# A hybrid DeepNorm layer: TensorE's order of the hyena stage emitted by a count of work instead of by the scheduler

## Chip, cores, metric

One core of a Trainium2 chip runs the whole program. The metric is the device time of one execution, in microseconds, shown as the median of several runs. TensorE (PE) does the matrix products, VectorE (DVE) and ScalarE (ACT) the elementwise work, GpSimd (POOL) the subtractions that split weights, and SyncE (SP) issues nearly all loads and stores.

## What is computed

One encoder layer (sequence 1024, model width 1024, all float32). Two token mixers read one combined projection of the normalised input; the part that the change touches is the second, the hyena branch. Cut to that, the reference reads:

```python
h = _layer_norm(x) * (1.0 + scale) + shift
p = h @ w_in + b_in                      # q, k, v | gate | hyena | gate | merge gates
u = centred_conv3(p_hy, conv_w, conv_b)
v, x1, x2 = jnp.split(u, 3, axis=-1)
filters = implicit_filters(S, ...)       # 3 sine layers of width 64, a product with w4, a decay
z = v
for o, gate_o in enumerate((x1, x2)):
    z = gate_o * (bidirectional_long_conv(z, filters[:, o, 0], filters[:, o, 1]) + filt_bias[o] * z)
y_hy = z * jax.nn.silu(g_hy)
```

The long convolution is a circular one of size 2048 by Fourier transforms. Behind the branches come two projections, sigmoid merge gates from the same `p`, an output projection, and a second normalisation.

## The kernel before

Precision: every projection splits both factors into a high and a low part and makes three products, wh·hTh, wh·hTl and wl·hTh. One projection tile (128 output columns for all 1024 positions) is two halves of 8 k-tiles by three products, that is 48 matmuls of 128x512 (`proj`, matmul on L242). Its weights come by one 512 KB load on SP (`load_w`, L229), are rounded by ScalarE (L222) and subtracted by GpSimd (`split_w`, L223). Names in the rows: `pj` is the PSUM tile of a projection, `hTh`/`hTl` the split input, `wh`/`wl` the split weights.

Stages: normalisation and adaLN up to about 61 us of the span; the hyena stage, to about 657 us, where attention's first score product (L859, tile `ss`) is issued; attention; the output stage from about 1240 us.

The hyena stage holds, beside 28 projection tiles of its own (12 for the inputs x, 12 early merge gates, 4 output gates) and the first tiles of attention:

- `hidden`: the sine layers of the filters, for two halves of two directions. A product on TensorE (L357, L359), then a range reduction on VectorE and a sine on ScalarE (L362 to L368), three times; the last result is split into `hid` (L374, L375).
- `gen_filter`, four times, for channel half hc and order o: eight pairs of products `px` = hid·w4 (L560, L561), each multiplied on VectorE by a decay table `dk` (L563) that SP loads into one of two buffers (L556); then butterflies (L447, L459) and a forward transform in eight frequency groups, j = -1 to 6 (`split_product`: `z` on L509 for j = -1, on L521 else), whose results `hs` are stored.
- `conv_order`/`long_conv`, four times in a row, each fed by the one before: for each frequency group a forward product `z` (L531 in plain float32 for j = -1, else L521), a product with the filter's spectrum on VectorE (L625, L627, then L447), a split into `yh`, `yl` (L499 on ScalarE, L500 on VectorE, signs on L511 and L512), an inverse product (L521), and butterflies into the result, which multiplies x (L693).
- `conv_to_rows`: one x tile is projected, copied (L591, L596), filtered by eight shifted multiply-adds on VectorE (`y`, L608), and transposed on TensorE (L612) into `xx` (L613). `gate_r` projects an early merge gate, `silu_tile`/`out_gate` an output gate.

Order: the tile scheduler orders all engines. It takes the emission order below as priorities; `conv_order` stands in `tc.high_priority(offset=HIGH)`, so that the convolutions' instructions go first and projections fill between them. The fills are placed by the driving calls at L719 to L749 with FILLS = (3, 1, 4, 4) and GATES = (0, 3, 2), the numbers of early gates emitted at each place. The products' tables `tcon0` and `tcon` are loaded at L730 to L733, into memory that the filters' pools free.

## Time and profile before

| | us |
|---|---|
| median of 3 runs (lowest, highest) | 1461.28 (1456.95, 1463.21) |
| the profiled execution | 1466.4 |
| its span | 1464.6 |
| PE busy | 1351.3 (92%) |
| DVE busy | 957.6 (65%) |
| ACT busy | 624.4 (43%) |
| POOL busy | 282.2 (19%) |

The span is the time between the first and the last recorded instruction of the profiled execution; its own time is 1.8 us longer. Times in rows count from the span's start. Busy shares of TensorE are those of pipelined matmuls, so a matmul's own duration is longer than the distance between two of them.

### The profile page before, as it was taken

How to read it: one execution, taken by the hardware profiler on the slowest of the kernel's cores; microseconds unless marked ns; L12 is line 12 of the kernel's file. 1: busy time of each engine (PE TensorE's matmuls, PEld its weight loads, DVE VectorE, ACT ScalarE, POOL GpSimd, SP SyncE). 2: the span in 40 equal slices, each digit the busy share in tenths (PEclk: the TensorE clock that was granted, in tenths of full speed). 3: DMA queues.
4: the chain of work that ended last, by engine and by line, in shares of the span. 5: the costliest groups of instructions: out<-in, count | busy, mean ns of one | idle time of the engine just before them, and what ended most of it. 6: DMA issues, size and time to landing. Idle time of an engine off the chain costs nothing.

```text
span 1464.6 us, 18389 instructions
## 1 busy us (share of the span) xinstructions
PE 1351.3 (92%) x6707; PEld 1098.4 (75%) x6707; DVE 957.6 (65%) x1709; ACT 624.4 (43%) x1220; POOL 282.2 (19%) x160
## 2 busy tenths in 40 slices
PE   4788979889899999999999999999999999689997
PEld 1467767767777777788988788878887888567886
DVE  4798768767999898745156714761466144288866
ACT  1544444534244443446355534663466343242110
POOL 1221121210113122141121112111211111231220
PEclk9799999999999999999999999999999999899999
DMA  9633544332112222121113421311131114588523
GB/s 255 182 97 105 175 133 149 110 130 79 54 58 69 87 65 79 58 84 30 44 59 116 103 61 58 92 30 43 59 91 31 44 58 123 184 249 220 158 88 72
DMA packets 157024, 145.86 MB, mean 100 GB/s; under 512 B 16611, under 2 KB 126591, under 8 KB 156678
## 3 DMA queue, kind: packets, MB, share of 16 engines
q1 hardware_dynamic: 156486, 140.44, 32.7%
q0 software_dynamic: 288, 4.19, 0.8%
q8 instruction: 53, 0.87, 0.3%
q14 instruction: 37, 0.30, 0.1%
q10 hardware_dynamic: 160, 0.06, 0.0%
HBM read 116.73 MB, written 27.92 MB: 99 GB/s over the span
## 4 chain that ended last, share of the span: by engine, by line
PE 64%; DVE 11%; DMA 5%; ACT 3%; issue 2%; POOL 1%; SPq 0%; DVEq 0%; ACTq 0%; POOLq 0%
PE pj L242 33%; PE pj L888 6%; PE z L521 6%; PE po L1138 6%; PE pj L1103 4%; PE po L929 2%; PE pp L922 2%; DVE iv L447 2%; DVE f L447 1%; DMA dk<-in_t_dec 1%; DMA wor<-in_w_out 1%; PE z L531 1%; PE ss L859 1%; DVE f L459 1%; DVE q L447 1%
## 5 line engine op out<-in xcount | busy, mean ns | idle before, releaser
L223 POOL TENSOR_TENSOR wl<-wr,wh 128x1024 fp32r<-128x1024 f32 x88 | 234.8, 2668 | 966.9 <-ACT wh L222 895.7
L242 PE MATMUL pj<-hTh,wh 128*128 128x512 f32 x1024 | 407.5, 398 | 4.0 <-ACT hTh L433 4.0
L242 PE MATMUL pj<-hTl,wh 128*128 128x512 f32 x1024 | 407.1, 398 | 1.5 <-POOL hTl L435 0.8
L242 PE MATMUL pj<-hTh,wl 128*128 128x512 f32 x1024 | 408.1, 399 | 0.0
L242 PEld LDWEIGHTS pj<-hTl,wh 128*128 128x128 f32 x1024 | 194.3, 190 | 40.5 <-DVE hTl L435 2.2
L242 PEld LDWEIGHTS pj<-hTh,wh 128*128 128x128 f32 x1024 | 194.4, 190 | 39.9 <-ACT hTh L433 4.1
L242 PEld LDWEIGHTS pj<-hTh,wl 128*128 128x128 f32 x1024 | 194.4, 190 | 37.3 <-issue 1.0
L222 ACT CAST wh<-wr 128x1024 fp32r<-128x1024 f32 x88 | 92.4, 1050 | 239.5 <-PE pj L242 82.3
L499 ACT CAST yh<-f 128x512 fp32r<-128x512 f32 x88 | 54.1, 615 | 105.2 <-DVE f L447 93.9
L899 DVE TENSOR_TENSOR tmp<-pj,bv 128x512 f32<-128x512 f32 x16 | 11.1, 692 | 115.0 <-PE pj L888 115.0
L500 DVE TENSOR_TENSOR yl<-f,yh 128x512 fp32r<-128x512 f32 x88 | 65.6, 756 | 22.2 <-ACT yh L499 19.9
L521 PE MATMUL z<-yh,tcon 128*128 128x512 f32 x224 | 65.7, 411 | 8.6 <-ACT yh L499 8.6
L918 ACT ACTIVATE sx<-sx,stat 128x256 f32<-128x256 f32 (+1 forms) x128 | 71.6, 563 | 3.1 <-DVE stat L916 3.0
L916 DVE CUSTOM_DVE_ANT_0 sx<-ss,tab 128x384 f32<-128x384 f32 (+1 forms) x112 | 53.7, 492 | 29.2 <-PE ss L844 18.0
L888 PE MATMUL pj<-wh,hTh 128*128 128x256 f32 x256 | 72.7, 284 | 0.0
L888 PE MATMUL pj<-wl,hTh 128*128 128x256 f32 x256 | 72.6, 284 | 0.0
L888 PE MATMUL pj<-wh,hTl 128*128 128x256 f32 x256 | 72.6, 284 | 0.0
L925 DVE TENSOR_TENSOR pt<-pp,pt 128x256 fp32r<-128x256 f32 (+1 forms) x128 | 61.8, 486 | 14.9 <-ACT pt L924 13.6
L1103 PE MATMUL pj<-yh,wl 128*128 128x512 f32 x128 | 52.0, 406 | 17.8 <-ACT yh L1084 11.3
L924 ACT CAST pt<-pp 128x256 fp32r<-128x256 f32 (+1 forms) x128 | 52.2, 425 | 33.4 <-PE po L929 28.9
L922 PE MATMUL pp<-ident,sx 128*128 128x128 f32 x320 | 58.3, 280 | 4.2 <-DVE pt L925 2.7
L521 PEld LDWEIGHTS z<-yh,tcon 128*128 128x128 f32 x224 | 40.6, 191 | 22.3 <-ACT yh L499 15.0
(236 smaller groups left out, 2546.2 us busy)
## 6 DMA issues: line engine op xcount, KB each, us to landing
wr<-in_w_in SPq DMA_DIRECT2D x64, 512.0 KB
xt<-in_x SPq DMA_DIRECT2D x32, 256.0 KB
wa<-in_w_ada SPq DMA_DIRECT2D x16, 512.0 KB
dk<-in_t_dec SPq DMA_DIRECT2D x32, 256.0 KB
r_d<-thr SPq DMA_DIRECT2D x32, 256.0 KB
h_dram<-hs SPq DMA_DIRECT2D x32, 256.0 KB
ht<-h_dram SPq DMA_DIRECT2D x32, 256.0 KB
thr<-r_d SPq DMA_DIRECT2D x32, 256.0 KB
```

What stands on the lines that cost most here:

```text
L222: ACT.copy(wh[:, :k, :], src)
L223: PO.tensor_tensor(wl[:, :k, :], src, wh[:, :k, :].bitcast(F32), ALU.subtract)
L242: PE.matmul(ps, w[:, kt, :], h[:, kt, sl], start=i == 0, stop=i == len(ops) - 1)
L447: V.tensor_tensor(o, a, b, op)
L500: V.tensor_tensor(yl[:, c, :], y, yh[:, c, :].bitcast(F32), ALU.subtract)
L521: PE.matmul(z, m, v, start=k == 0, stop=k == 5)
L888: PE.matmul(ps[:, t % 2], h[:, 4 * q + k, P * t : P * t + P], w[:, 2 * k : 2 * k + 2, :], start=first and t % 2 == 0 and i == 0, stop=last ...
L918: ACT.activation(sx[:, : n * P], sx[:, : n * P], AF.Exp, bias=stat[:, t, e, 0:1], scale=-1.0, accum_out=stat[:, t, e, 1:2])
L922: PE.transpose(pp[:, a * P : (a + 1) * P], sx[:, a * P : (a + 1) * P], ident)
L925: V.tensor_tensor(pt[:, :n, 1, :], blk(pp), pt[:, :n, 0, :].bitcast(F32), ALU.subtract)
L1103: PE.matmul(ps, w[:, 4 * b + kt, :], y[:, kt, :], start=i == 0, stop=i == len(ops) - 1)
L1138: PE.matmul(po, m[:, P * q : P * q + P], w[:, kt, ds_], start=n == 0, stop=n == 23)
```

## The change

Around the hyena stage, TensorE's instructions are put under `tc.manual_schedule`: TensorE then issues them exactly in the order in which the program emits them, while the other engines are still ordered by the scheduler. The emission keeps two counts, `clk["pe"]` and `clk["dve"]`, of the work emitted so far for TensorE and for VectorE. Before each transform product and each filter product it calls `pace()`, which pulls projection work from a queue, three matmuls at a time, until TensorE's count reaches 1.1 times VectorE's plus 1 us. The queue is filled by `push_x`, `push_gates` and `push_out`; transposes of an x tile are put off to the next tile's middle. In `long_conv` the inverse product of group j - 1 and the butterflies of j - 2 are emitted behind the forward product of group j. `high_priority` and FILLS are gone, GATES holds six numbers. `split_w` takes an engine as an argument, and no call gives one, so the weight splits stay on GpSimd. The work itself is the same: the same products, loads and elementwise operations.

```diff
-FILLS = (3, 1, 4, 4)
-GATES = (0, 3, 2)
+
+GATES = (0, 4, 2, 2, 0, 4)
+RATIO = 1.1
+LAG = 1.0
...
+    def split_w(src, eng=None):
 
         k = src.shape[1]
+        eng = eng or PO
...
+    clk = {"pe": 0.0, "dve": 0.0}
+
+    def cols_of(ap):
+        n = 1
+        for k in ap.shape[1:]:
+            n *= k
+        return n
+
+    def dve(ap):
+        clk["dve"] += 0.14 + 0.001065 * cols_of(ap)
+
+    def pe(n, passes=1):
+        clk["pe"] += 0.0133 + passes * n / 2400
...
+    def prefetch(n0):
+        if n0 not in ready:
+            w = load_w(w_in[:, n0 : n0 + P])
+            ready[n0] = split_w(w)
+
+    def pull():
+
+        while now or queue:
+            if not now:
+                now.append(queue.pop(0)[1]())
+            if next(now[0], None):
+                return True
+            now.clear()
+        while deferred:
+            for _ in deferred.pop(0)():
+                pass
+        return False
+
+    def pace(lag=LAG):
+        while clk["pe"] < RATIO * clk["dve"] + lag and pull():
+            pass
+
+    def proj_steps(n0, evac):
+
+        prefetch(n0)
+        wh, wl = ready.pop(n0)
+        for half in range(2):
+            ps = ps_w.tile([P, 512], F32, name="pj", tag="mm")
+            sl = slice(512 * half, 512 * half + 512)
+            ops = [(w, h, kt) for kt in range(KT) for w, h in ((wh, hTh), (wh, hTl), (wl, hTh))]
+            for i, (w, h, kt) in enumerate(ops):
+                PE.matmul(ps, w[:, kt, :], h[:, kt, sl], start=i == 0, stop=i == len(ops) - 1)
+                pe(512)
+                if i % 3 == 2:
+                    yield True
+            if half == 0:
+                if queue:
+                    prefetch(queue[0][0])
+                while deferred:
+                    yield from deferred.pop(0)()
+            evac(half, ps, cols[:, BIN + n0 // P : BIN + n0 // P + 1])
...
-        def split_product(j, y, tab, inverse, pool):
-
-
-            z = ps_z.tile([P, 2, W], F32, name="z", tag="z")
+        def split_y(j, y, inverse, pool):
+
             yh, yl = [pool.tile([P, 3, W], F32R, name="y" + q, tag="y" + q, bufs=2) for q in "hl"]
             at = int(inverse)
             c, n = slice(at, at + 2), 2 - 2 * at
             ACT.copy(yh[:, c, :], y)
             V.tensor_tensor(yl[:, c, :], y, yh[:, c, :].bitcast(F32), ALU.subtract)
+            dve(y)
+            if j >= 0:
+                ACT.mul(yh[:, n, :], y[:, at, :], -1.0)
+                ACT.mul(yl[:, n, :], yl[:, 2 * at, :].bitcast(F32), -1.0)
+            return yh, yl
+
+        def split_product(j, parts, tab, inverse):
+
+
+            pace()
+            z = ps_z.tile([P, 2, W], F32, name="z", tag="z")
+            yh, yl = parts
...
+                    pace()
                     for m in range(2):
                         hs = hid[e][:, a // 2, P * m : P * m + P]
                         PE.matmul(px[:, m, :], hs, wh, start=True, stop=False)
                         PE.matmul(px[:, m, :], hs, wl, start=False, stop=True)
+                        pe(2 * W)
                     b = a + 8 * e
                     V.tensor_tensor(g[:, b : b + 2], px, dk, ALU.mult)
+                    dve(dk)
...
+            def turn():
+                if "x" not in x:
+                    x["x"] = pool.tile([P, 8, W], F32, name="xx", tag=tag, bufs=bufs)
+                for q in range(2):
+                    px = ps_x.tile([P, 512], F32, name="px", tag="px")
+                    for a in range(4):
+                        PE.transpose(px[:, a * P : (a + 1) * P], y[:, (4 * q + a) * P : (4 * q + a + 1) * P], ident)
+                        pe(P, 2)
+                    ACT.copy(x["x"][:, 4 * q : 4 * q + 4, P * c : P * c + P], px.rearrange("p (a c) -> p a c", a=4))
+                    yield True
+                x["left"] -= 1
+
+            deferred.append(turn)
...
-                v = conv_product(j, p1, True)
+                return p1
+
+            def inverse(j, p):
+                v = conv_product(j, conv_split(j, p, True), True)
...
+            r, p = {}, None
+            for j, y in stage1(x[:, 0:4], x[:, 4:8], x, quad("s"), quad("d"), quad("q")):
+                z = conv_product(j, conv_split(j, y, False), False)
+                if j >= 0:
+                    inverse(j - 1, p)
+                if j > 0:
+                    butterflies(j - 2)
+                p = spectrum(j, z)
+            inverse(6, p)
+            butterflies(5)
+            butterflies(6)
...
         def conv_order(x, z, hc, o):
 
-            with tc.high_priority(offset=HIGH):
-                for a, y in long_conv(z, hc, o):
-                    V.tensor_tensor(x[:, a], y, x[:, a], ALU.mult)
-            return x
-
-        def out_gate(z, hc):
-            for c in range(2):
+            for a, y in long_conv(z, hc, o):
+                xt = need(x)
+                V.tensor_tensor(xt[:, a], y, xt[:, a], ALU.mult)
+                dve(y)
+            return need(x)
...
-        x0 = conv_x(0, 0)
-        gen_filter(0, 0)
-        x1 = conv_x(0, 1)
-        gen_filter(0, 1)
-        fill(GATES[0])
-        gen_filter(1, 0)
-        fill(GATES[1])
-        gen_filter(1, 1)
-        fill(GATES[2])
...
-        z = conv_order(x1, x0, 0, 0)
-        x2 = conv_x(0, 2, "xx2")
-        fill(FILLS[0])
-        z = conv_order(x2, z, 0, 1)
-        x0 = conv_x(1, 0)
-        x1 = conv_x(1, 1)
...
+        with tc.manual_schedule(engines={PE.engine}):
+            clk.update(pe=0.0, dve=0.0)
+            x0 = push_x(0, 0)
+            push_gates(GATES[0])
+            x1 = push_x(0, 1)
+            push_gates(GATES[1])
+            for hc, o in ((0, 0), (0, 1), (1, 0), (1, 1)):
+                gen_filter(hc, o)
+                note(("filter", hc, o))
+            need(x1)
+            fpool.close()
+            hy = st.enter_context(tc.tile_pool(name="hy", bufs=1, reuse_waits="tile", side="right"))
+            tcon0 = hy.tile([P, 8, P], F32, name="tcon0")
+            SY.dma_start(tcon0, A["t_con0"])
+            tcon = hy.tile([P, 28, P], F32R, name="tcon")
+            PO.dma_start(tcon, A["t_con"])
+            hy2 = st.enter_context(tc.tile_pool(name="hy2", bufs=2, reuse_waits="tile", side="right"))
+            x2 = push_x(0, 2, "xx2")
+            push_gates(GATES[2])
+            z = conv_order(x1, need(x0), 0, 0)
+            note("conv 0 0")
+            x0 = push_x(1, 0)
+            push_gates(GATES[3])
+            z = conv_order(x2, z, 0, 1)
+            note("conv 0 1")
+            x1 = push_x(1, 1)
+            need(x0)
+            og = push_out(z, 0)
+            push_gates(GATES[4])
+            x2 = push_x(1, 2, "xx2")
+            z = conv_order(x1, need(x0), 1, 0)
+            note("conv 1 0")
+            need(og)
+            push_gates(GATES[5])
+            z = conv_order(x2, z, 1, 1)
+            note("conv 1 1")
+            push_out(z, 1)
+            push_gates(N_EARLY)
+            while pull():
+                pass
```

Three places on TensorE, as the order of instructions shows them. In these rows a line number, the operation, what it writes and reads, and the tile's size stand; "x4" is four alike in a row.

The sine layers, before: TensorE around the third pair of products (L359), with projection matmuls (`pj`) of the first x tiles and early gates and the transposes of the first x tile (L612) between them.

```order
L242 MATMUL pj<-hTh,wl 128x512
L242 MATMUL pj<-hTh,wh 128x512
L359 MATMUL px<-f,w_124 128x512
L242 MATMUL pj<-hTl,wh 128x512
L242 MATMUL pj<-hTh,wl 128x512
L242 MATMUL pj<-hTh,wh 128x512
L242 MATMUL pj<-hTl,wh 128x512
L359 MATMUL px<-f,w_124 128x512
L612 MATMUL px<-ident,y 128x128 x4
L242 MATMUL pj<-hTh,wl 128x512
```

The same place with the change: the last matmuls of the first projection, all six sine-layer products (L407, L409), and the first filter products.

```order
L288 MATMUL pj<-hTl,wh 128x512
L288 MATMUL pj<-hTh,wl 128x512
L407 MATMUL px<-feat,w_125 128x512 x2
L409 MATMUL px<-f,w_124 128x512 x4
L630 MATMUL px<-w4h,hid 128x256
L631 MATMUL px<-w4l,hid 128x256
L630 MATMUL px<-w4h,hid 128x256
L631 MATMUL px<-w4l,hid 128x256
L288 MATMUL pj<-hTh,wh 128x512
```

Ahead of the first filter product (`px<-w4h,hid`) TensorE had 153 projection matmuls and 16 transposes; now it has 9 projection matmuls and none of the transposes.

The products of the first filter, before: a stretch of the eight pairs, with fills of projection matmuls.

```order
L560 MATMUL px<-w4h,hid 128x256
L561 MATMUL px<-w4l,hid 128x256
L242 MATMUL pj<-hTh,wh 128x512
L242 MATMUL pj<-hTl,wh 128x512
L242 MATMUL pj<-hTh,wl 128x512
L242 MATMUL pj<-hTh,wh 128x512
L242 MATMUL pj<-hTl,wh 128x512
L242 MATMUL pj<-hTh,wl 128x512
L242 MATMUL pj<-hTh,wh 128x512
L242 MATMUL pj<-hTl,wh 128x512
L242 MATMUL pj<-hTh,wl 128x512
L242 MATMUL pj<-hTh,wh 128x512
```

With the change, in the same eight pairs:

```order
L630 MATMUL px<-w4h,hid 128x256
L631 MATMUL px<-w4l,hid 128x256
L288 MATMUL pj<-hTh,wh 128x512
L288 MATMUL pj<-hTl,wh 128x512
L288 MATMUL pj<-hTh,wl 128x512
L630 MATMUL px<-w4h,hid 128x256
L631 MATMUL px<-w4l,hid 128x256
L630 MATMUL px<-w4h,hid 128x256
L631 MATMUL px<-w4l,hid 128x256
```

The eight pairs now hold three fills of 3 projection matmuls in this filter, and two of 3 in each of the other three, where fills of 1 to 12 stood.

The end of the second convolution, before: TensorE at a forward product (six matmuls, four with `yh` and two with `yl`), an inverse product behind it, the fill, and the next pair.

```order
L242 MATMUL pj<-hTl,wh 128x512
L242 MATMUL pj<-hTh,wl 128x512
L242 MATMUL pj<-hTh,wh 128x512
L521 MATMUL z<-yh,tcon 128x512 x4
L521 MATMUL z<-yl,tcon 128x512
L242 MATMUL pj<-hTl,wh 128x512
L242 MATMUL pj<-hTh,wl 128x512
L242 MATMUL pj<-hTh,wh 128x512
L521 MATMUL z<-yl,tcon 128x512
L242 MATMUL pj<-hTl,wh 128x512
L242 MATMUL pj<-hTh,wl 128x512
L242 MATMUL pj<-hTh,wh 128x512
```

The end of the same convolution with the change: forward 5, inverse 4, forward 6, inverse 5 and inverse 6.

```order
L583 MATMUL z<-yh,tcon 128x512 x4
L583 MATMUL z<-yl,tcon 128x512 x2
L583 MATMUL z<-yh,tcon 128x512 x4
L583 MATMUL z<-yl,tcon 128x512 x2
L583 MATMUL z<-yh,tcon 128x512 x4
L583 MATMUL z<-yl,tcon 128x512 x2
L583 MATMUL z<-yh,tcon 128x512 x4
L583 MATMUL z<-yl,tcon 128x512 x2
L583 MATMUL z<-yh,tcon 128x512 x4
L583 MATMUL z<-yl,tcon 128x512 x2
L288 MATMUL pj<-hTh,wh 128x512
```

The last five products follow each other with no projection between them, since the queue was empty there; the 72 projection matmuls come behind them.

## Rows read from the trace of the kernel before

**Rows 1.** Windows view, the filter part of the stage: busy, clock, DMA share, GB/s.

```profile
115.90:302.30 186.40, 163.02 (x748) 131.04 (x747) 143.14 (x210) 83.89 (x161) 35.41 (x21) 0.94 0.46 147
```

**Rows 2.** Timeline, the bounds of the three parts: start us, us, engine, line.

```profile
61.43 0.79 PE L242 MATMUL pj<-hTh,wh 128*128 128x512 f32 x1 [4.01 <-ACT hTh L433]
...
115.91 0.41 PE L560 MATMUL px<-w4h,hid 128*128 128x256 f32 x1
...
302.31 3.75 PE L531 MATMUL z<-f,tcon 128*128 128x256 f32 x8 [5.06 <-DMA tcon<-in_t_con]
...
657.07 0.28 PE L859 MATMUL ss<-ks,qs 128*128 128x256 f32 x1
```

**Rows 3.** Timeline of TensorE, fill behind a forward product and the next product.

```profile
485.48 0.39 PE L242 MATMUL pj<-hTh,wl 128*128 128x512 f32 x1
...
489.12 0.39 PE L521 MATMUL z<-yh,tcon 128*128 128x512 f32 x1
```

**Rows 4.** Timeline of TensorE, eight transposes of an x tile.

```profile
113.62 1.07 PE L612 MATMUL px<-ident,y 128*128 128x128 f32 x8 [2.63 <-DVE y L608]
```

**Rows 5.** Windows view of VectorE in the sine chain.

```profile
79.60:110.20 30.60, 30.43 (x56) 1.00 0.37 116
```

**Rows 6.** Groups by line of VectorE, 79 to 110 us: busy, mean ns.

```profile
L608 DVE SCALAR_TENSOR_TENSOR y<-u,cols,y 128x192 f32<-128x192 f32 (+3 forms) x13 | 8.1, 641 | 0.0
```

**Rows 7.** Timeline of VectorE behind the sine chain.

```profile
108.78 1.39 DVE L375 TENSOR_TENSOR hid<-f,hid 64x512 fp32r<-64x512 f32 x2
...
117.01 0.69 DVE L563 TENSOR_TENSOR g<-px,dk 128x512 f32<-128x512 f32 x1 [3.06 <-PE px L561]
```

**Rows 8.** Windows view of VectorE, the four filter-product phases.

```profile
117.00:131.40 14.40, 11.68 (x21) 0.95 0.57 156
164.10:177.60 13.50, 8.73 (x13) 1.00 0.54 158
202.90:221.30 18.40, 10.06 (x17) 0.98 0.62 190
244.00:258.90 14.90, 9.23 (x14) 1.00 0.64 207
```

**Rows 9.** Windows view, line L242 alone, the first and third of these phases.

```profile
117.00:131.40 14.40, 10.53 (x39) 7.16 (x39) 0.95 0.57 156
...
202.90:221.30 18.40, 8.38 (x33) 5.86 (x33) 0.98 0.62 190
```

**Rows 10.** Tile view of dk: the products L563, and what VectorE waited for.

```profile
L563 DVE TENSOR_TENSOR g<-px,dk x32: 671/691/692, 117.0 to 258.2; 128x512 f32<-128x512 f32 x32
...
  DMA dk<-in_t_dec: 17.8, 13
```

**Rows 11.** Waits of TensorE, 60 to 660 us: us, times, longest.

```profile
PE z L521 <- ACT yh L499: 15.5, 8, 3.7
PE z L531 <- DVE f L447: 8.0, 3, 4.2
PE z L509 <- ACT yh L499: 6.6, 4, 2.0
```

**Rows 12.** Timeline of VectorE, L625 of two successive frequency groups.

```profile
485.68 0.69 DVE L625 TENSOR_TENSOR f<-z,ht 128x512 f32<-128x512 f32 x1 [1.50 <-PE z L521]
...
492.10 0.69 DVE L625 TENSOR_TENSOR f<-z,ht 128x512 f32<-128x512 f32 x1 [1.60 <-PE z L521]
```

**Rows 13.** Timeline of VectorE at a convolution's end.

```profile
530.87 1.29 DVE L447 TENSOR_TENSOR iv<-v,z 128x512 f32<-128x512 f32 x2 [1.65 <-PE z L521]
...
550.58 0.74 DVE L447 TENSOR_TENSOR f<-f 128x256 f32<-128x256 f32 x2
```

**Rows 14.** Windows view, a gap of TensorE and the stretch behind it.

```profile
195.00:200.20 5.20, 1.52 (x7) 0.94 (x5) 1.90 (x3) 1.71 (x4) 1.04 (x2) 1.00 0.42 152
200.20:203.60 3.40, 3.35 (x8) 2.68 (x9) 3.19 (x5) 1.86 (x5) 0.00 (x0) 0.50 0.31 114
```

More of the change, by code (lines that the diff above doesn't have):

```diff
@@ L51 @@
 RES = (12, 14, 6, 15, 7, 11, 3)
-HIGH = 20000
 def _split(t):
@@ L500, in split_product @@
             V.tensor_tensor(yl[:, c, :], y, yh[:, c, :].bitcast(F32), ALU.subtract)
+            dve(y)
[7 more added lines that the diff above has]
+            yh, yl = parts
+            at = int(inverse)
             if j < 0:
@@ L557, in gen_filter @@
                     wh, wl = w4[e]
+                    pace()
                     for m in range(2):
@@ L608, in conv_to_rows @@
                 V.scalar_tensor_tensor(a, b, w[k], a, ALU.mult, ALU.add)
-            for q in range(2):
-                px = ps_x.tile([P, 512], F32, name="px", tag="px")
-                for a in range(4):
-                    PE.transpose(px[:, a * P : (a + 1) * P], y[:, (4 * q + a) * P : (4 * q + a + 1) * P], ident)
-                ACT.copy(dst[:, 4 * q : 4 * q + 4, co : co + P], px.rearrange("p (a c) -> p a c", a=4))
+                dve(a)
+            def turn():
[10 more added lines that the diff above has]
+            deferred.append(turn)
         def long_conv(x, hc, o):
@@ L639, in long_conv, with butterflies @@
                 vs[j] = v
+            def butterflies(j):
+                v = vs[j]
                 if j == 0:
@@ L705, in out_gate, with push_gates @@
                         PE.transpose(px[:, a * P : (a + 1) * P], z[:, 4 * q + a, P * c : P * c + P], ident)
+                        pe(P, 2)
                     view = lambda t: t.rearrange("p (r t i) -> p t r i", r=16, t=8)[:, 4 * q : 4 * q + 4].rearrange(
                         "p t r i -> p r t i")
-                    V.tensor_tensor(view(yh), px.rearrange("p (t r i) -> p r t i", t=4, r=16), view(sg), ALU.mult)
+                    V.tensor_tensor(view(yh), px.rearrange("p (t r i) -> p r t i", t=4, r=16), view(sgs[0]), ALU.mult)
+                    dve(px)
+                    yield True
                 SY.dma_start(yh_d[ft], yh)
+                left["left"] -= 1
+            for c in range(2):
+                queue.append((C_GH + P * (2 * hc + c), lambda c=c: steps(c)))
+            return left
         early = iter(range(N_EARLY))
-        def fill(n):
+        def push_gates(n):
             for _ in range(n):
@@ L744, in hybrid_encoder, with note @@
-        z = conv_order(x1, x0, 1, 0)
-        fill(FILLS[2])
-        z = conv_order(x2, z, 1, 1)
-        fill(FILLS[3])
-        out_gate(z, 1)
-        fill(16)
+                    n0, evac = gate_evac(j, lambda: hx.tile([P, 512], F32, name="thr", tag="thr", bufs=2))
+                    queue.append((n0, lambda n0=n0, evac=evac: proj_steps(n0, evac)))
+        def note(what):
+            if DEBUG:
+                print(what, {k: round(v, 1) for k, v in clk.items()}, "queued", len(queue), "now", len(now))
@@ new lines, in hybrid_encoder @@
+        with tc.manual_schedule(engines={PE.engine}):
[37 more added lines that the diff above has]
+            while pull():
+                pass
+            note("end")
```

104 lines of the change are left out of this document (56 added, 48 removed).

## The prediction

> **What bounds the kernel now.** I read first the busy shares, then the hyena stage in windows, then what TensorE waits for there, then single stretches of the timeline. TensorE is busy 92% of the span and VectorE 65%, as the table ahead shows; in the filter part of the stage they stand at 163.0 and 143.1 us of 186.4 [rows 1]. There neither engine alone is the bound: time is lost where TensorE has nothing that it may issue. So I price TensorE's work in the stage and look for the difference to the clock on the wall.
>
> Prices: 16 projection matmuls fill the 3.64 us from 485.48 to 489.12, so one costs 0.2275 us, and a transform product of 128x512 the same [rows 3]. A transpose of 128x128 costs 1.07 / 8 = 0.134 [rows 4]. A filter-product or L509 matmul of 128x256 is half of 0.2275, 0.113. The plain float32 products stand at 3.75 / 8 = 0.47 us a record in a slow stretch [rows 2]; I set 0.43 for each of the 32 that the order counts, 0.86 for the six sine products, which are twice as wide. The last two are estimates, and alike before and after.
>
> By these prices and the counts of the order, TensorE has 42.1 us of work between its first projection matmul (61.43) and the first filter product (115.91): 153 projection matmuls, 16 transposes, 6 sine products. It has 147.6 from there to the first convolution product (302.31), and 319.4 from there to attention's first score product (657.07), 509.1 in all [rows 2]. The wall times are 54.5, 186.4 and 354.8 us. So TensorE loses 12.4, 38.8 and 35.4 us: 86.6 in all. That is what an order can win. The change has the same 509.1 us in the stage, divided otherwise: 7.2, 154.6 and 347.3. Everything behind 657 us is the same work in the same order, and I let it shift as a whole.
>
> **The sine chain.** VectorE is the bound there: it works 30.43 of 30.60 us up to 110.2 [rows 5]. 8.1 us of it are taps of the first x tiles (L608) that stand between the chain's steps [rows 6]. The change projects only 9 matmuls before the chain, so no x tile is ready and these taps leave the chain. Its end moves from 110.2 to 102.1. Without them VectorE stands between the steps while ScalarE takes its sine; I add 2.6 us for that (an estimate: six steps, less than half a 0.69-us operation each, since the two halves alternate). The 5.8 us between the chain's end at 110.17 (1.39 from 108.78) and the first filter product's matmul came from projections and transposes queued ahead of it [rows 2, 7]; now these products stand next in TensorE's order, as the order's second fence shows, and w4 is there. I allow 0.6: they begin at 105.3 instead of 115.9, 10.6 earlier. But TensorE has done 7.2 us of work by then, not 42.1: it is 34.9 behind, net **24.3 us the wrong way** (bounds: 2.6 better if VectorE never stands; 4 worse if it stands for a whole 0.69-us operation at twelve steps, six in each direction).
>
> **The filter products.** Four phases of eight products, each from 13.5 to 18.4 us long [rows 8]. In these TensorE was given 39 projection matmuls in the first and 33 in the third [rows 9], and hid most of VectorE's waits. Now there are 9 in the first and 6 in each of the others. With 32 matmuls of 0.113 a phase holds 5.1 us of TensorE's work. How long will it be? VectorE waits 17.8 us for the decay tables in the four [rows 10], the two buffers and SP's loads are the same, and the products on VectorE cost 0.69 each as before. I take the middle of the four lengths, 14.65 us (14.4 and 14.9), since no row says that the loads come sooner. So TensorE loses 9.5 us a phase, 38 in all. Ends: at VectorE's own busy time, 9.9 on average [rows 8], it loses 4.8 a phase, 19 in all; at the longest phase, 18.4, it loses 53.
>
> To this come the first transform product of each filter, which waits for ScalarE's split, 6.6 us in four [rows 11], and the tables of the convolution, whose load TensorE awaited 5.06 us [rows 2] behind about as long a fill as now (31 projection matmuls before, 30 now). 105.3 + 154.6 + 38 + 6.6 + 5.1 = **309.6** for the first convolution product, 7.3 later than 302.3.
>
> **The convolutions.** A forward product's inverse can start 3.64 us after the forward product has been issued, and VectorE takes 6.42 us from one group to the next when it is the bound (485.68 to 492.10) [rows 3, 12]. The old order was already pipelined by one group: forward and inverse of neighbouring groups stand together, with fills of 13 to 18 between the pairs, as the third place in the order shows. Now a pair (2.7 us of TensorE) is followed by fills of 9, 30, 3, 42, 9, 21 and none. After a long fill VectorE is one group ahead, and a short one costs only 3.64 - 2.73 less the fill; after a short one the next costs 6.42 - 2.73 less its fill. So 12 behind 9 costs 1.0 (12 matmuls are 2.7 us), an empty place behind a long fill 0.9, behind an empty one 3.7, and an inverse 6 straight behind inverse 5, 3.64 - 1.36 = 2.3. Over the four convolutions I count 1, 6, 2 and 5, together 14. The splits that TensorE waits for in convolutions add some 4 us, a quarter of the 15.5 of [rows 11]. **18 lost** in place of 35.4. What goes away is real: VectorE's butterflies at a convolution's end take 19.7 us to the next first input (530.87 to 550.58) [rows 13], and TensorE ran dry there three times, 8.0 us [rows 11]; the new fills there hold 22 to 30 us. Ends: 4 us lost if VectorE stays ahead; 35.4 if nothing improves.
>
> Waits that I cost at nothing: weights. Each tile's load and split are now emitted half a tile ahead, 24 x 0.2275 = 5.5 us of TensorE, and they hide behind that and the waits above; no wait of a projection for weights stands among TensorE's largest [rows 11]. GpSimd keeps the same subtractions. If the cover went, each of the tiles could stall for part of one split.
>
> On the strictness of TensorE's order: behind a waiting transform product everything stands still, as TensorE's wait of up to 3.7 us for `yh` shows [rows 11]. The whole sum above treats fills as fixed for that reason.
>
> **Sum.** 309.6 + 347.3 + 18 = 674.9 for attention's first score product, against 657.1: 17.8 later. The profiled execution took 1466.4 us, 5.1 more than the median of the runs, 1461.3. 1466.4 + 17.8 - 5.1 = **1479 us**, 1.2% slower. What a measurement here can tell from no change is about 0.5%, 7.3 us: faster is under 1454, slower over 1468.6.
>
> **Rivals.**
> - *Filter products at VectorE's pace: faster.* Place: the four phases. If the decay tables are no longer waited for, because SP's loads stand alone in a phase with few weights, and VectorE holds nothing but the eight products, a phase takes 8 x 0.69 = 5.5 us, and TensorE loses 0.4 a phase: 36.6 us better, 1442. It decides from a phase of 8.4 us down. For it: 17.8 us of waits could go. Against: VectorE was busy 8.7 us and more in each phase, and the DMA engines' share was already above a half [rows 8]. Chance 0.2.
> - *Phases at VectorE's busy time, 9.9 us: no change.* 19 us better than the sum, 1460; or the convolutions lose only 4 and the phases are a bit shorter. Chance 0.2.
> - *The clock goes down in the thinner stretches: slower still.* From 195.0 to 200.2 TensorE was busy 1.52 of 5.2 us, and in the 3.4 us behind it the granted clock was 0.50, its lower level of 1.2 GHz, so half of 3.4 us was lost [rows 14]. The sine chain (now nearly empty of matmuls) and each filter phase (5.1 of 14.65 us) are as thin: five places at 1.7 us, 8.5, which gives 1487. Against: the old order has such stretches too, and part of the loss falls where TensorE would wait anyway. Chance 0.18. The Trainium skill, "TensorE: Matmul & The Clock Gate", section "HAM oscillation — how this bites in real kernels", says that idle gaps drop the clock and that each burst of matmuls behind a gap starts cold, once for every gap; that speaks against gathering the fills into long runs, and by it the time is 1487 rather than 1479. The trace agrees as far as the two rows just named go.
> - *The convolutions lose what they lost, 35.4 us,* since VectorE's order, still the scheduler's, and TensorE's fixed one wait for each other in turn: 17.4 worse, 1496. For it: uneven fills. Against: the ends are better covered. Chance 0.15.
> - That the change does not do what it says is only a matter of places: the order shows fills that follow the count, and none where the queue is empty, at the end of the second convolution. That is in the sum.
>
> **Chances and range.** My forecast 0.27, the four rivals 0.2, 0.2, 0.18, 0.15. Slower 0.27 + 0.18 + 0.15 = 0.6, same 0.2, faster 0.2. The range leaves out half of the faster rival's chance below 1447, and the sum of the last two rivals, 1505, above 1500.
>
> **What would show it.** Right: TensorE stands nearly still between 70 and 105 us, the first L630 product starts near 105; the phases of `g` keep 13 to 18 us and hold under 10 projection matmuls; the first convolution product near 310; waits for `f` at L598 gone; attention's first score product near 675. Wrong: phases of `g` under 9 us, a first convolution product before 300, or a stage that ends before 660.

## The result, and the profile after

The change made the kernel slower: 1543.11 us median of 4 runs (1539.51 to 1547.78) against 1462.24 (1456.95 to 1463.77), a ratio of 1.0562 with a 95% interval of 1.052 to 1.0603. That is 80.9 us. The direction was forecast, the size was not: the forecast of 1479 had 18 us, and its range ended at 1500.

The first part of the page of the changed kernel, busy time and share of the span:

```profile
PE 1370.4 (89%) x6707; PEld 1115.4 (72%) x6707; DVE 954.7 (62%) x1709; ACT 626.3 (41%) x1220; POOL 263.3 (17%) x160
```

The windows view of the changed kernel, the three parts of the stage (sine chain, filters, convolutions). The columns: window, its length, busy us (and instructions) of PE, PEld (weight loads), DVE, ACT and POOL, granted clock of TensorE, DMA share, GB/s. [rows 1] has the second part before.

```profile
55.40:96.20 40.80, 14.18 (x22) 5.69 (x22) 37.77 (x68) 16.83 (x25) 5.61 (x4) 0.58 0.33 104
96.20:308.60 212.40, 178.82 (x781) 145.27 (x782) 148.86 (x221) 87.46 (x167) 26.08 (x21) 0.90 0.38 125
308.60:730.70 422.10, 374.24 (x1571) 296.49 (x1572) 289.13 (x498) 159.41 (x292) 63.03 (x32) 0.94 0.21 64
```

The sine chain and the convolutions of the kernel before:

```profile
61.40:115.90 54.50, 46.94 (x181) 33.71 (x182) 52.33 (x87) 29.91 (x44) 12.98 (x7) 0.94 0.32 99
...
302.30:657.10 354.80, 334.35 (x1445) 264.53 (x1446) 284.66 (x489) 148.43 (x280) 70.57 (x29) 0.98 0.23 71
```

The stage's work is the same and VectorE's busy time in the convolutions is nearly so (289 us, 285 before), but they take 422 us in place of 355. Behind attention's first score product nothing changed: 1539.0 - 730.7 = 808.3 us to the end, 807.5 before.

For every run I use the forecast's own measure: the wall time of a part less the work that TensorE's order holds there, at the forecast's prices. That is what TensorE loses in the part (us). Two runs whose filter parts have the same order on TensorE, VectorE and ScalarE (`read_u` and `read_u_even` below) differ there by 5 us, so less than that says nothing.

| | sine chain | filters | convolutions | sum |
|---|---|---|---|---|
| before | 12.4 | 38.8 | 35.4 | 86.6 |
| forecast | 36.7 | 49.7 | 18 | 104.4 |
| the change | 33.6 | 57.9 | 74.7 | 166.2 |

166.2 - 86.6 = 79.6 us, the measured difference to 1.3. (The profiled execution happened to enter the stage 6 us earlier than the one before, first projection at 55.4 against 61.4; so parts are compared, not times from the span's start.) Half of it, 39.3, lies in the convolutions, where the forecast had a gain of 17.

What TensorE and VectorE waited for in the convolutions, the waits view: us in all, times, longest. First TensorE before (the convolutions' part of [rows 11]) and with the change:

```profile
PE z L521 <- ACT yh L499: 8.6, 6, 1.9
PE z L531 <- DVE f L447: 8.0, 3, 4.2
PE z L531 <- DMA tcon<-in_t_con: 5.1, 1, 5.1
PE z L521 <- DVE yl L500: 3.7, 4, 1.3
```

```profile
PE px L692 <- DVE y L683: 26.5, 5, 12.8
PE z L583 <- ACT yh L549: 14.6, 11, 3.5
PE z L598 <- DMA tcon<-in_t_con: 6.5, 1, 6.5
PE z L583 <- DVE yl L550: 5.5, 5, 2.2
```

then VectorE, before and with the change:

```profile
DVE f L625 <- PE z L521: 22.1, 15, 2.1
...
DVE f L625 <- PE z L531: 7.5, 3, 5.6
```

```profile
DVE f L710 <- PE z L598: 32.1, 4, 15.7
DVE f L710 <- PE z L583: 28.9, 15, 4.8
```

The wait for `tcon` ends with the first convolution product, so its time lies in the filters. A wait that was not there before leads the list: the transposes of an x tile (L692) wait for VectorE's taps (L683). And each engine waits for the other: VectorE stood 32.1 us for the four first products L598 (7.5 us for L531 before). The longest pair of such waits, the end of the third convolution, in the timeline of the changed kernel; VectorE:

```profile
591.73 1.28 DVE L805 TENSOR_TENSOR xx<-iv,xx 128x512 f32<-128x512 f32 x2
592.94 1.01 DVE L683 SCALAR_TENSOR_TENSOR y<-u,cols,y 128x768 f32<-128x768 f32 x1
...
596.79 1.81 DVE L683 SCALAR_TENSOR_TENSOR y<-u,cols,y 128x7 f32<-128x7 f32 x5
598.52 2.42 DVE L497 TENSOR_TENSOR q<-xx 128x1024 f32<-128x1024 f32 x3
616.62 0.69 DVE L710 TENSOR_TENSOR f<-z,ht 128x512 f32<-128x512 f32 x1 [15.68 <-PE z L598]
```

and TensorE:

```profile
585.37 0.39 PE L288 MATMUL pj<-hTh,wl 128*128 128x512 f32 x1
598.60 1.73 PE L692 MATMUL px<-ident,y 128*128 128x128 f32 x7 [12.85 <-DVE y L683]
...
614.46 0.39 PE L288 MATMUL pj<-hTh,wl 128*128 128x512 f32 x1
614.69 1.89 PE L598 MATMUL z<-f,tcon 128*128 128x256 f32 x8
```

These rows show two waits in a row, each while the other engine works. VectorE runs the convolution's final butterflies, and its order has the taps behind them. TensorE has reached the transposes that need these taps and stands for 12.85 us, with 57 projection matmuls behind them that need nothing from VectorE. When the transposes are through, TensorE does these 57, and VectorE, which has finished the next input by then, stands 15.68 us for the product behind them. The fill was meant to cover VectorE's butterflies; it ran after them.

### The profile page after: what moved, and what is told of

Read it like the earlier page. It is cut to its first block, busy times and chain, and to the rows that moved or that the text cites. A ratio compares the mean times of both kernels' runs of the same rounds, so it can differ in the third digit from the quotient of the medians.

```text
span 1539.0 us, 18393 instructions
## 1 busy us (share of the span) xinstructions
PE 1370.4 (89%) x6707; PEld 1115.4 (72%) x6707; DVE 954.7 (62%) x1709; ACT 626.3 (41%) x1220; POOL 263.3 (17%) x160
## 4 chain that ended last, share of the span: by engine, by line
PE 63%; DVE 19%; DMA 7%; ACT 5%; issue 4%; POOL 1%; SPq 0%; DVEq 0%; ACTq 0%; POOLq 0%
PE pj L306 24%; PE pj L288 9%; PE pj L1040 6%; PE z L583 5%; PE po L1290 5%; PE pj L1255 4%; DVE y L683 3%; PE po L1081 2%; PE pp L1074 2%; DMA xt<-in_x 2%; DVE iv L497 2%; DVE f L497 2%; DMA dk<-in_t_dec 2%; DMA wor<-in_w_out 2%; DVE yl L550 1%
## 5 line engine op out<-in xcount | busy, mean ns | idle before, releaser
L228 POOL TENSOR_TENSOR wl<-wr,wh 128x1024 fp32r<-128x1024 f32 x88 | 219.8, 2498 | 1073.7 <-ACT wh L227 977.1
L306 PE MATMUL pj<-hTh,wh 128*128 128x512 f32 x576 | 227.9, 396 | 0.0
L288 PE MATMUL pj<-hTh,wh 128*128 128x512 f32 x448 | 184.5, 412 | 4.4 <-ACT hTh L483 4.4
L288 PEld LDWEIGHTS pj<-hTh,wl 128*128 128x128 f32 x448 | 88.0, 196 | 19.4
L550 DVE TENSOR_TENSOR yl<-f,yh 128x512 fp32r<-128x512 f32 x88 | 69.2, 793 | 36.3 <-ACT yh L549 33.8
L583 PE MATMUL z<-yh,tcon 128*128 128x512 f32 x224 | 65.2, 414 | 14.7 <-ACT yh L549 14.6
```

The lines of the kernel that those rows point to most:

```text
L228: eng.tensor_tensor(wl[:, :k, :], src, wh[:, :k, :].bitcast(F32), ALU.subtract)
L288: PE.matmul(ps, w[:, kt, :], h[:, kt, sl], start=i == 0, stop=i == len(ops) - 1)
L306: PE.matmul(ps, w[:, kt, :], h[:, kt, sl], start=i == 0, stop=i == len(ops) - 1)
L550: V.tensor_tensor(yl[:, c, :], y, yh[:, c, :].bitcast(F32), ALU.subtract)
L583: PE.matmul(z, m, v, start=k == 0, stop=k == 5)
```

## The experiments

Line numbers of edited kernels shift by some lines; the waits are told by tile. A diff marked "in part" leaves out lines of the edit.

**read_u: the transposes' wait taken away.** The transposes read the projected tile instead of the filtered one. The taps are still computed, but not used: the short convolution is left out of what follows.

```diff
-                        PE.transpose(px[...], y[:, ...], ident)
+                        PE.transpose(px[...], u[:, ...], ident)
```

> The transposes of an x tile read the projected tile u instead of the filtered y, so TensorE no longer waits for VectorE's taps; the taps are still computed, but their result is not used (the short convolution is left out of what follows). Theory A (transposes at a fixed place in TensorE's order wait for taps that VectorE does late, 34.0 us in nine waits, and the clock falls behind the longest of them): the waits go and some 5 to 10 us of clock with them, 1495 to 1510 us. Rival B (the fills between products are too uneven, the transposes only stand where TensorE would wait anyway): within 8 us of 1543.

Measured: 1507.57 us, 35.5 below the change. The convolutions lose 46.5 us in place of 74.7, the filters 54.3. The wait is gone from TensorE's list, and 28.2 us with it in the convolutions: 26.5 us of waiting for taps go, 4.8 come back as waits for `yh` (14.6 to 19.4), and the lower clock level costs some 6 less (an estimate, worked out under "The clock" below). Theory A holds, and it is not the whole.

**late, prio, late_prio: the same wait mended, with the whole computation.** Later in TensorE's order, earlier in VectorE's (in part; these lines stood without the `with`), and both.

```diff
-            if half == 0:
-                if queue:
-                    prefetch(queue[0][0])
+            if half == 0 and queue:
+                prefetch(queue[0][0])
+            if half == 1:
                 while deferred:
                     yield from deferred.pop(0)()
```

```diff
+            with tc.high_priority(offset=20000):
+                ACT.activation(y, u, AF.Identity, scale=w[1], bias=...)
...
+                    V.scalar_tensor_tensor(a, b, w[k], a, ALU.mult, ALU.add)
```

> Same as the change, but an x tile's transposes stand behind the second half of the next tile's matmuls instead of behind the first: 24 matmuls or 5.5 us later in TensorE's order. Theory A: of the nine waits, what is under 5.5 us goes, some 26 of 34 us, 1515 to 1525. Rival B: no change, 1535 to 1550.

> Same as the change, but the taps and the ScalarE operation ahead of them have the priority that the convolutions had before, so VectorE does them as soon as the projection is there. Theory A: waits for taps fall from 34 us to under 10, 1505 to 1520; what the convolution chain loses by up to 4 us of taps in its way is smaller. Rival B: the chain is later by the taps and nothing is won, 1540 to 1560.

> Both measures on the transposes at once: 5.5 us later in TensorE's order, and the taps ahead of the convolution's work on VectorE. Measured alone they gave 21 and 19 us. If the waits for taps are one cause with two remedies, nearly all of it goes and the time comes near the one without the wait at all (1507.6): 1503 to 1512. If taps that go first delay the convolutions as much, no better than the two alone: 1518 to 1528.

Measured: 1521.81, 1524.51 and 1510.83 us; for `prio` that is 4.5 more than theory A had allowed. The waits view of the convolutions in `late`, in `prio`, and the longest two in `late_prio`:

```profile
PE px L692 <- DVE y L683: 9.9, 1, 9.9
```

```profile
PE px L693 <- DVE y L684: 14.6, 5, 5.2
```

```profile
PE z L583 <- ACT yh L549: 14.5, 9, 3.5
PE z L598 <- DVE f L497: 6.8, 2, 3.6
```

Alone each takes about half of the wait or more (26.5 us in the change), both together all of it, though TensorE now stands 6.8 us for the next input `f` at L598, and the time comes within 3.3 us of the run without the wait. So some 32 us of the 81 are this one dependence.

**free, conv_free, filt_free: who orders TensorE.** The same emission with TensorE left to the scheduler, throughout or in one part.

```diff
-        with tc.manual_schedule(engines={PE.engine}):
+        with ExitStack():
```

> Same emission, but TensorE's order is left to the scheduler again (no manual schedule); the pipelined convolution and the queue stay. If the fixed order is what costs (A and B are both forms of it), it comes back to 1455 to 1480. If the new emission itself is the cause (no priority for the convolutions, pipelining by one group, fewer projections early), it stays above 1510.

> TensorE's order is fixed up to the end of the filters and left to the scheduler from the first convolution on. By the two traces the change is 39 us behind the kernel before in the convolutions (74.8 us of TensorE's time lost there against 35.4) and 34 us in sine chain and filters (6.3 us later with 27.9 us less work done). If the two parts add up: 1543 - 39, that is 1500 to 1510. If the convolutions only suffer from what the filters left undone (the queue), it stays above 1525.

> The other way round: the scheduler orders TensorE in sine chain and filters, and the order is fixed from the first convolution on. If the parts add up: 1543 - 34, that is 1505 to 1515. If the filters' loss is made up later anyway, 1535 to 1545.

Measured: 1456.24 us for `free` (ratio to before 0.9972, 0.9954 to 0.9991); 1492.25 for `conv_free`, 50.9 below the change; 1502.47 for `filt_free`, 40.6 below. Both partial runs came out somewhat better than expected (1500 and 1505 at best). What the scheduler orders loses about what it lost before, what stays fixed loses about what it lost with the change (us):

| | sine chain | filters | convolutions |
|---|---|---|---|
| free | 12.4 | 38.8 | 34.4 |
| conv_free | 33.4 | 52.0 | 33.4 |
| filt_free | 12.4 | 42.5 | 73.4 |

The windows view of the filter part in `filt_free`, and of the convolutions in `conv_free`:

```profile
102.40:274.10 171.70, 143.67 (x671) 114.32 (x671) 142.30 (x211) 82.75 (x162) 26.66 (x19) 0.94 0.44 141
```

```profile
305.30:682.90 377.60, 358.17 (x1556) 286.88 (x1557) 288.84 (x498) 158.85 (x291) 72.81 (x32) 0.97 0.23 72
```

TensorE's waits in the convolutions of `conv_free`:

```profile
PE px L692 <- DVE y L683: 12.3, 4, 4.3
PE z L598 <- DMA tcon<-in_t_con: 5.6, 1, 5.6
PE z L583 <- ACT yh L549: 5.3, 4, 1.5
```

Pipelining by one group, the queue and the early gates' numbers, which `free` keeps, do no harm and hardly any good. Even the scheduler's order waits for taps, 12.3 us in the convolutions of `conv_free`, less than half of the change's 26.5. The two parts add up: 50.9 + 40.6 = 91.5, against 86.9 with both left to the scheduler (`free`), and the intervals of these two-run ratios are about 1% wide on either side.

**phase: fills moved into the filter-product phases.** This tests the forecast's largest term.

```diff
-                    pace()
+                    for _ in range(2 if e else 1):
+                        pull()
```

> The same as the change, but the eight filter products of each filter carry 36 projection matmuls in small fills (3 and 6 by turns) in place of 9 or 6; these come out of the long fill behind the products, and the rest of TensorE's order is alike. The recorded forecast put 9.5 us of TensorE's time lost into each phase, 38 us in all; with 36 matmuls (8.2 us) in it a phase would lose some 3: 20 to 28 us of these 38 come back, 1515 to 1525. Rival: VectorE is the bound of the whole filter part, the long fill behind the products covered VectorE's butterflies and these waits now appear there: 1535 to 1545.

Measured: 1542.26 us, no change. The filters lose 54.7 in place of 57.9, within the 5 us that like runs differ by. The waits view of TensorE in the filters of `phase`, and of the change:

```profile
PE z L572 <- ACT yh L549: 15.3, 3, 7.1
PE px L631 <- DVE g L635: 9.0, 4, 4.2
```

```profile
PE px L630 <- DVE g L634: 14.3, 12, 3.8
...
PE z L572 <- ACT yh L549: 4.4, 2, 2.5
```

The waits for the products shrink by 5 us, and the wait of the first transform product behind them grows by 11. That is the rival's account, that the long fill behind the phase had covered VectorE's butterflies, and its time came out.

**head: the next filter's first products earlier** (in part).

```diff
             for j, y in stage1(u, g[:, 8:12], g, g[:, 12:16], u, g[:, 8:12]):
+                if j == 5 and following:
+                    ahead.append(start(*following))
                 z = split_product(j, split_y(j, y, False, fl3), tabf, False)
```

The ground for it, VectorE at a filter's end in the changed kernel's timeline, with 4.32 + 0.99 + 3.36 + 4.06 us of standing:

```profile
202.05 0.69 DVE L550 TENSOR_TENSOR yl<-f,yh 128x512 fp32r<-128x512 f32 x1 [4.32 <-ACT yh L549]
203.74 0.69 DVE L550 TENSOR_TENSOR yl<-f,yh 128x512 fp32r<-128x512 f32 x1 [0.99 <-ACT yh L549]
207.79 1.29 DVE L634 TENSOR_TENSOR g<-px,dk 128x512 f32<-128x512 f32 x2 [3.36 <-PE px L631]
...
213.46 1.37 DVE L634 TENSOR_TENSOR g<-px,dk 128x512 f32<-128x512 f32 x2 [4.06 <-DMA dk<-in_t_dec]
```

> The same as the change, but the first two products of the next filter are emitted ahead of a filter's last two pairs of transform products, as the scheduler places them, so that VectorE finds its next work. Theory (at each filter's end VectorE is idle for some 12 us, waiting for splits that wait for products behind fills, and then for the next filter's first products): 4 to 6 us at each of three ends, 12 to 18 us, 1525 to 1531. Rival (what VectorE wins there it waits for at the next fill): 1537 to 1547.

Measured: 1530.8 us (1525.63 and 1535.97), 12.3 below the change, with a ratio to before of 1.0368 to 1.0542, which overlaps the change's. The filters lose 48.9, 9 less; `read_u_even`, without this edit, lost 49.0 there. So that this is a piece of the filters' loss is likely and not shown.

**sine, read_u_sine, lp_head_sine: work for TensorE in the sine chain.** Two early gates are emitted between the sine products, and two fewer in the fourth convolution; in the last of the three on top of `late_prio` and `head`. The sine products come under the written order with them, and the weights loaded ahead of the stage are these gates' (in part):

```diff
+        with tc.manual_schedule(engines={PE.engine}):
+            hidden()
...
+                    cover_pull(8 if l else 0)
```

> The same as the change, but two early merge gates (96 projection matmuls, 21.8 us of TensorE) are emitted between the products of the sine layers, 24 ahead of each of the last four, and two fewer in the fourth convolution. If TensorE's stand in the sine chain costs what the forecast said (work not done while VectorE is the bound), 18 to 24 us come back: 1519 to 1525. Rival: the sine chain gets longer by as much, because each of its products now waits behind 5.5 us of projections: 1535 to 1545.

> The wait for taps away (transposes read u; the short convolution is left out of what follows) and two gates moved into the sine chain. Moved alone, these 21.8 us of TensorE's work won 4 us, since the convolutions, which then had 21.8 us less to do, took only 8 less. Theory: what the convolutions waited for there was the transposes, not TensorE's work; without that wait less work counts, 1488 to 1496 (12 to 20 below 1507.6). Rival: the convolutions are held by the waits between products and VectorE's chain anyway: 1500 to 1508.

> Fixed order with transposes later, taps first, the next filter's first products early (these two measured 32 and 12 us alone, together some 1499), and two gates in the sine chain. If TensorE's work in the sine chain counts once the waits are mended, 1480 to 1489. If it does not (the convolutions then lack what fills them), 1495 to 1503.

Measured: 1538.64, 1504.48 and 1505.38 us: of 21.8 us, 4 won against the change and 3 against `read_u`. The third run is 5 below `late_prio`, but it has `head`'s edit as well, and no run has `late_prio` and `head` alone; it stands 2 us above the range in which this work does not count. In `sine` the chain, from the first projection to the first filter product, takes 6.1 us longer (61.68 to 108.53, 46.8 against 40.7) and loses 19.5 us (33.6 in the change), but the convolutions lose 88.6. The rival's time came out for `sine`, its reason (a chain longer by as much) in part. The windows view of the convolutions in `sine`:

```profile
320.50:734.60 414.10, 354.60 (x1474) 278.46 (x1475) 285.22 (x498) 154.95 (x285) 60.25 (x30) 0.94 0.20 60
```

With 21.8 us less to do they take 8 less, and the longer chain takes most of that back. I had expected this to change once the transposes' wait was gone. It hardly did (10.6 us less in `read_u_sine`, 383.3 against 393.9, and a chain 5.4 longer): that theory falls. In the fixed order a projection taken out of a convolution leaves a hole (TensorE's wait for `yh` there: 14.6 us in the change, 25.2 in `sine`, 30.0 in `read_u_sine`). Whether gates taken out of the filters' fill would have been a gain was not tried.

**read_u_even: even fills in the convolutions**, 21 matmuls ahead of each forward product, on top of `read_u` (the short convolution is left out there too).

> The wait for taps away as before, and in the convolutions 21 projection matmuls ahead of each forward product in place of what the count asks for (3 to 45); the total at each convolution's start is the same. With the wait away the convolutions still lose 46.5 us of TensorE's time, 13 more than when the scheduler orders them (33.4), and TensorE waits 19.4 us for yh in place of 5.3. If the uneven fills are that remainder, 8 to 14 us go: 1494 to 1500. If not (what remains lies at the convolutions' ends): 1503 to 1510.

Measured: 1504.26 us, 3.3 below `read_u`, within what two runs can tell. By the trace the convolutions lose 40.1 in place of 46.5; the wait for `yh` did not shrink (23.0 us, 19.4 in `read_u`). Uneven fills are a small part at most; 5 us of the run's gain lie in the filters, which the edit does not touch.

**joint0, filt_free_lp: do the parts add up?** All remedies at once in the fixed order, without the sine chain (18 matmuls ahead of each forward product); and the scheduler in chain and filters with late_prio in the convolutions.

> Everything tried on the fixed order at once, with all of the computation: transposes later, taps first, 36 fills in each filter phase, even fills in the convolutions, the next filter's first products early. If these are the places where the fixed order loses in filters and convolutions, what is left is the sine chain: 1475 to 1490. If each only moves a wait to the next place, no better than transposes alone (1510.8): 1500 to 1515.

> The scheduler's order in sine chain and filters (alone 1502.5, 41 below the change) together with the two measures on the transposes in the fixed order of the convolutions (alone 1510.8, 32 below). If the two are separate causes they add up: 1543 - 41 - 24 to 32 (some of the 32 lay in the filters), 1470 to 1480. If they overlap: above 1490.

Measured: 1507.4 and 1490.94 us, both short of the sum. In `joint0` filters and convolutions lose 46.3 and 49.6, hardly less than with single remedies (48.9 in `head`, 46.8 in `late_prio`). In `filt_free_lp` the convolutions keep their 47.1, but the scheduler's own filter part, now with taps that go first and transposes that go later, loses 56.6 in place of 42.5; some 9 of these 14 us are time at the lower clock level (an estimate, as under "The clock"). So the remedies do not add up; which wait each moves where was not followed up.

**free_prio, free_head, free_late: the scheduler's order with the pieces that helped.**

> Scheduler orders TensorE, new emission, and the taps with priority. In the run with the scheduler's order TensorE still waited 12.9 us for taps. If these waits lie on the way: 1444 to 1452, faster than both kernels. If VectorE's taps then delay the convolutions as much: 1454 to 1464.

> Scheduler orders TensorE, new emission with the next filter's first products early. The scheduler already places them so; if it does no better with the hint: 1453 to 1460, as without. If it had not yet gone far enough: 1445 to 1451.

> Scheduler orders TensorE, new emission with the transposes behind the second half. TensorE waited 12.9 us for taps in the scheduler's order without this. If the scheduler's model was too hopeful about the taps, the later place wins 4 to 8 us: 1448 to 1453. If it shifts them itself: 1453 to 1460.

Measured: ratios to the kernel before of 1.0006 (0.9973 to 1.0039), 1.0 (0.9976 to 1.0023) and 0.9989 (0.9966 to 1.0013). None of them takes away the waits for taps that remain in the scheduler's order: over the stage 12.9 us in `free`, 15.4 in `free_prio`, 12.4 in `free_head`, and 8.6 in `free_late`, where the wait for `f` at L598 grows from 3.1 to 7.7. So whether these waits are on the way stays open. No version beats the kernel before by more than `free`'s 0.3%.

## Why the prediction was wrong

- **The step that failed is the convolutions' term**, "18 lost in place of 35.4". Measured: 74.7. The forecast counted a convolution's end as covered by fills of 22 to 30 us, and put TensorE's wait for the taps of an x tile at nothing: it priced the transposes as work and did not ask when the taps they need are done on VectorE, whose order has them behind the very butterflies that the fill should cover. That wait is 26.5 us, and without it the convolutions lose 28.2 us less (`read_u`). VectorE then stands in its turn while TensorE makes up the fill (32.1 us for L598). The forecast's own remark, that everything stands still behind a waiting transform product, was not applied to a waiting transpose. The rest, 46.5 in `read_u` against 33.4 when the scheduler orders the convolutions, is not one cause: TensorE stands 25.4 us for the splits `yh` and `yl` in `read_u` and 5.9 in `conv_free`, which in turn stands 12.3 for taps. With even fills the convolutions lost 6.4 of these 13 less; the remainder is open.
- **The sine chain was right**: from its first projection to the first filter product 40.7 us (96.15 - 55.43) with 7.2 of work, 33.6 lost against 36.7. The direction of the forecast rests on it, so that was not luck. A slip inside it did no harm: six steps of less than half of 0.69 us are 2.1 us at most and not 2.6, and twelve whole ones are 8.3, which is 5.7 worse and not 4. But its price is not settled: the forecast took TensorE's work put off there as due later in full, and in `sine` and `read_u_sine` two gates put into the chain made it 5 to 6 us longer and the convolutions, with 21.8 us less to do, only 8 to 11 shorter.
- **The filters** came out at 57.9 lost, 49.7 forecast. The four phases are as long as forecast (14.8, 12.9, 16.2 and 12.8 us against 14.65 each); the mechanism is wrong. They were to lose 38 us for want of fills, and with 36 matmuls in each of them (`phase`) the filters lose 54.7: the wait moves behind the phase. What bounds the part is in the waits of VectorE and TensorE for each other; which of these decides is not shown, and `head`'s 9 us are a hint. With the scheduler's order this part loses 42.5 with less work left in it (129.2 us of TensorE, 154.5 in the change).
- **Rivals.** The faster one (phases at VectorE's pace) and the one at VectorE's busy time (9.9 us) are out: a phase takes 12.8 to 16.2 us (first of `g` to last, 97.5 to 111.6, 153.4 to 165.6, 207.8 to 223.3, 253.8 to 265.9, each with 0.7 for the last). The slower one on the convolutions, "VectorE's order, still the scheduler's, and TensorE's fixed one wait for each other in turn", had the right mechanism at less than half its size: it let them lose what they had lost before as a limit, and nothing in the trace set that limit. The range was too narrow for the same reason: the upper bounds of its terms were taken from the old order, which is the thing that was changed. That the first convolution product started at 308.6, near the forecast's 309.6, is luck: the profiled execution entered the stage 6 us early.
- **The clock.** The trace bears out the rival on the clock, which at 8.5 us was too small; it comes on top of the waits. The granted clock was 0.58, 0.90 and 0.94 in the three parts, against 0.94, 0.94 and 0.98 before. By the trace's records of the granted clock, TensorE was busy for 85 us of the stage at the lower level, 1.2 GHz (12, 37 and 36 us in the parts), and for 40 us in the kernel before (6, 19 and 15). Two projection matmuls start 0.43 us apart there (601.20 and 601.62) and 0.2275 at full rate, so about half of that time is lost: 43 us against 20, some 22 of the 80 (an estimate, and an upper one, since part of it falls where TensorE would have waited anyway). In the convolutions TensorE's waits (without `tcon`) are 47.5 us against 20.3 and the lower level costs 18 against 8, which together make 37 to 38 of their 39.3. The row that the rival rested on, [rows 14], shows a wait too and not thin work: TensorE was busy until 196.5 and then stood 3.72 us for `yh`:

```profile
200.25 2.50 PE L521 MATMUL z<-yh,tabf 128*128 128x512 f32 x5 [3.72 <-ACT yh L499]
```

  Behind the wait of 12.85 us in the changed kernel the granted clock was 0.66 from 598.6 to 605.4 us. The Trainium skill, "TensorE: Matmul & The Clock Gate", section "HAM oscillation — how this bites in real kernels", has bursts behind gaps start cold; the trace agrees in this place, where the row is:

```profile
598.60:605.40 6.80, 6.80 (x25) 5.75 (x26) 2.34 (x3) 1.17 (x2) 0.00 (x0) 0.66 0.01 2
```

  At full rate this stretch would have taken 4.5 us, so the wait of 12.85 cost 2.3 more. No run changes the clock alone.

## What to carry to other kernels

From one emission, the kernel took 1456 us with TensorE in the scheduler's order and 1543 with it in an order placed by a count of work. A count that keeps two engines level says nothing of latency: whoever writes the order of one engine has to ask of each instruction, transposes too, where its operand stands in the other engine's order, and put work that needs nothing ahead of it, not behind. And a stage in which two engines wait for each other was not priced well here as one engine's work plus stalls, since remedies that won 12 to 41 us alone did not add up; nor can the old order's losses serve as the worst case of a new one.

## What the runs showed of the hardware that was not expected

VectorE can be held up while GpSimd splits weights. In the changed kernel's timeline, first GpSimd, then VectorE:

```profile
581.30 2.41 POOL L228 TENSOR_TENSOR wl<-wr,wh 128x1024 fp32r<-128x1024 f32 x1 [16.72 <-ACT wh L227]
```

```profile
578.81 0.68 DVE L497 TENSOR_TENSOR iv<-iv 128x512 f32<-128x512 f32 x1
...
581.34 3.72 DVE L497 TENSOR_TENSOR iv<-iv 128x512 f32<-128x512 f32 x3
```

The first of the three additions, which begins with GpSimd's subtraction, takes 2.92 us, where one of its kind takes 0.68; it ends 0.55 us after the subtraction. Not every overlap costs that: of the 28 operations of this kind and size (TENSOR_TENSOR, 128x512 float32) in this trace that overlap a split, 11 took 2.0 to 2.9 us, and each of these ended 0.55 us after its split; the other 17 took 0.87 at most. So a split costs VectorE some 2.2 us where it holds up such an operation on its chain. Both kernels have the same 88 splits, and where they fall is not what the change altered; no run here moves them to another engine.
